# RWKV's second part as one pass over its chunks, and a 64-row product in both MLPs

## The chip, the cores and the metric

The kernel runs on one core of a Trainium2 chip. The metric is the device time of one execution in microseconds (us), less is better. Engines are named as the profile names them: PE (TensorE, matmuls) with PEld (its weight loads), DVE (VectorE), ACT (ScalarE), POOL (GpSimd) and SP (SyncE, which issues most loads). PE's two clock levels are 2.4 GHz (granted clock 1.00 in the rows) and 1.2 GHz (0.50).

## What is computed

Two layers of a decoder trunk on 256 tokens of width 2048, all in float32. The part that the change touches is layer 0, whose mixer puts sparse attention (NSA, 8 heads of 128) beside RWKV-7 (16 heads of 64), and the MLPs of both layers:

```
for layer in range(DEPTH):
    h = _rms_norm(x, norm_mix[layer])
    if layer % 2 == 0:
        u = h @ w_in_a[e]
        y_a = _nsa(u_nsa, ...)
        y_b = _rwkv7(u_rw, ...)
        y = jnp.concatenate([y_a, y_b], axis=-1) @ w_out_a[e]
    else: ...                                   # RG-LRU and HGRN2
    x = x + y
    x = x + _sq_relu_mlp(_rms_norm(x, norm_mlp[layer]), w_ff1[layer], w_ff2[layer])

def _rwkv7(...):                                # per head, state 64 x 64
    sa = einsum('bhij,bhj->bhi', state, a_t)
    state = state * w_t + sa * b_t + v_t * k_t
    y_t = einsum('bhij,bhj->bhi', state, r_t)
    ...
    y = ((y - mean) * lax.rsqrt(var + RW_LNX_EPS)) * lnx_w + lnx_b
    y = (y + bonus) * g

def _sq_relu_mlp(h, w1, w2):
    z = jax.nn.relu(h @ w1)
    return (z * z) @ w2
```

## The kernel before

**Projections and MLPs.** Activations lie transposed, channels on the 128 partitions, 256 tokens along a row. Each activation is held as two fp32r halves side by side (`hi|lo`, 512 columns), each weight is loaded as fp32 (512 KB a piece, issued by SP), cast on ACT to `wh` (L130) and its rest `wl` made on DVE (L132). A *unit* makes 128 output channels: 16 pairs of matmuls, each `wh` over 512 columns (L152) and then `wl` over 256 (L153). An MLP is 128 units, that is 2048 such pairs, and nothing else on PE but one mean-square product (L206) just ahead of it or in its first unit.

**Layer 0.** Up to about 310 us of the span PE runs the in-projection; `rwkv_a` makes, for each of 8 pairs of heads j, the operands of the chunked RWKV form (`rwp`, `pm`), writes them to DRAM, and gathers the 32x32 triangles `nb`, which DVE solves (`rw_solve`, L443 to L447) into `z_d` in DRAM. From about 310 to 466 us `rwkv_b` runs, four times, each for two pairs j and j+1: it loads `inv`, `pm`, `rwp` and `bg` (POOL issues these), makes the 64x64 inverses (`psh`, `psf`), and goes through 4 chunks of 64 tokens in turn: `psx` (state and scores times values), `psu` (the inverse applied), `pss` (state update), `psy` (output); at the end come the group norm (`pmn`, `pvr`) and the gate, into `yr`. Attention heads (lines above L555) and the units left over of the projection are interleaved. Then comes the out-projection (`mm_o`), the MLP of layer 0 (to about 1290), layer 1's mixer and out-projection (to about 1702) and its MLP.

**Order.** A scheduler fixes the order of each engine's instructions at build time, by dependences and priorities; on the chip each engine goes through its own in that order and waits where an operand is not there. Products of fp32 operands appear as two records each, fp32r ones as one. The size behind the buffers in a record, as `128*64`, is the part of the array (rows * columns) that it is set to; `128*128` is the whole.

Of the kernel before, what the change touches and what calls it, by code (L numbers as in the profile page):

```python
# [19 lines left out]
P = 128  # L20
# [34 lines left out]
RWP_N = 4 * 512 + 4  # L55
# [3 lines left out]
def kernel(  # L59
# [95 lines left out]
    def unit(src, mv, name, folded=False, tag=None, parts=None, pool=None):  # L155
# [76 lines left out]
    def layer0_mix():  # L232
        with ExitStack() as st:
            mx = st.enter_context(tc.tile_pool(name="mx", bufs=1))
            acc, hx = norm("a0")
            rwp_d = [dram.tile([P, 2, RWP_N], F32, name=f"rwp_d{j}") for j in range(4)]
            pm_d = [dram.tile([P, 2, 8, P], F32, name=f"pm_d{j}") for j in range(4)]
# [10 lines left out]
            with tc.tile_pool(name="pa", bufs=1) as pa:  # L248
# [39 lines left out]
                rwkv_a(pa, gate, hx, scaled_by(rstd), rwp_d, pm_d, nb, first, load_cw)  # L288
            with tc.tile_pool(name="pb", bufs=1) as pb, tc.tile_pool(name="pn", bufs=1) as pn:
                rw_solve(pb, nb, z_d)  # L290
                for j in range(0, 8, 2):
                    rwkv_b(pb, j, rwp_d, pm_d, z_d, yr)
# [17 lines left out]
    def rwkv_a(pa, gate, hx, scaled, rwp_d, pm_d, nb, first, load_cw):  # L310
# [26 lines left out]
        for j in range(8):  # L337
# [3 lines left out]
            rwp = tl("rwp", (P, RWP_N), 2, name=f"rwp_{j}")  # L341
            ar = rwp[:, 0:512].rearrange("p (c w t) -> p c w t", c=4, w=2)
            pm = tl("pm", (P, 8, P), 2, name=f"pm_{j}")
# [23 lines left out]
            A.copy(rwp[:, 1536:1540], w.rearrange("p (c t) -> p c t", c=4)[:, :, 63])  # L367
# [10 lines left out]
            with behind():  # L378
# [26 lines left out]
                V.tensor_mul(rwp[:, 1540:1796], psb[:, :T], v)  # L405
# [5 lines left out]
                A.copy(rwp[:, 1796:2052], psg[:, :T])  # L411
# [6 lines left out]
                A.copy(rwp[:, 1024:1536], ptv)  # L418
                A.copy(rwp[:, 512:1024], ptb)
# [6 lines left out]
                for q in range(2):  # L426
                    V.tensor_mul(
                        pm[:, 4 * q : 4 * q + 4], pps[q].rearrange("p (s t) -> p s t", s=4),
                        c_("pair")[:, None, :].to_broadcast([P, 4, P]))
                G.dma_start(pm_d[j // 2][:, j % 2], pm)  # L430
                for i in range(2):
                    G.dma_start(
                        nb[i * 64 + j * 8 : i * 64 + j * 8 + 8],
                        pm_d[j // 2][32 * i : 32 * i + 32, j % 2, :, 32 * i : 32 * i + 32].rearrange("s h t -> h s t"))
                G.dma_start(rwp_d[j // 2][:, j % 2], rwp)
# [14 lines left out]
    def rwkv_b(pb, j, rwp_d, pm_d, z_d, yr):  # L450


        def tl(tag, shape, bufs=1, name=None):
            return pb.tile(list(shape), F32, tag=tag, name=f"{tag}_{j}" if name is None else name, bufs=bufs)

        R = range(2)
        inv = tl("inv", (64, 2, 8, 64), 2)
        zat = tl("zat", (32, 2, 8, 32))
        pm = tl("pm", (P, 2, 8, P))
        rwp = tl("rwp", (P, 2, 1540))  # L460
        bg = tl("bg", (P, 2, 512))
        G.memset(inv, 0.0)
        inv16 = inv.rearrange("p r h t -> p (r h) t")
        for i in range(2):
            b0 = i * 64 + j * 8
            G.dma_start(inv16[32 * i : 32 * i + 32, :, 32 * i : 32 * i + 32], z_d[b0 : b0 + 16].rearrange("h r t -> r h t"))
        V.transpose(zat.rearrange("p r h t -> p (r h) t"), inv16[0:32, :, 0:32])
        G.dma_start(pm, pm_d[j // 2])
        G.dma_start(rwp, rwp_d[j // 2][:, :, 0:1540])
        G.dma_start(bg, rwp_d[j // 2][:, :, 1540:2052])  # L470
        ar = rwp[:, :, 0:512].rearrange("p r (c w t) -> p r c w t", c=4, w=2)
        bkt = rwp[:, :, 512:1024].rearrange("p r (c t) -> p r c t", c=4)
        uv = rwp[:, :, 1024:1536].rearrange("p r (c t) -> p r c t", c=4)
        wt, bv, gg = rwp[:, :, 1536:1540], bg[:, :, 0:256], bg[:, :, 256:512]
        psh = bank(f"psh_{j}")
        for r in R:
            for n in range(8):
                M.matmul(psh[32:64, (r * 8 + n) * 32 : (r * 8 + n + 1) * 32], pm[0:32, r, n, 32:64], zat[:, r, n], start=True, stop=True)
        hs_ = tl("hs", (64, 2, 8, 32))
        A.copy(hs_[32:64].rearrange("p r h t -> p (r h t)"), psh[32:64])  # L480
        psf = bank(f"psf_{j}")
        for r in R:
            for n in range(8):
                M.matmul(psf[0:32, (r * 8 + n) * 32 : (r * 8 + n + 1) * 32], hs_[32:64, r, n], inv[32:64, r, n, 32:64], start=True, stop=True)
        A.copy(inv[0:32, :, :, 32:64], psf[0:32].rearrange("p (r h t) -> p r h t", r=2, h=8))

        y = tl("y", (P, 2, T))
        y4 = y.rearrange("p r (c t) -> p r c t", c=4)
        s = None
        for c in range(4):  # L490
            psx = bank(f"psx_{j}_{c}")
            for r in R:
                if c:
                    M.matmul(psx[0:64, r * P : (r + 1) * P], ar[:, r, c, 0], s[:, r], start=True, stop=False)
                for h in range(2):
                    M.matmul(psx[0:64, r * P + h * 64 : r * P + h * 64 + 64], pm[64:128, r, 4 * h + c, 0:64],  # L496
                             uv[64:128, r, c, h * 64 : h * 64 + 64], start=c == 0, stop=c == 0 or h == 1)
            xv = tl("xv", (64, 2, P), name=f"xv_{j}_{c}")
            A.copy(xv.rearrange("p r t -> p (r t)"), psx[0:64, 0:T])
            psu = bank(f"psu_{j}_{c}")  # L500
            for r in R:
                for h in range(2):
                    M.matmul(psu[0:64, r * P + h * 64 : r * P + h * 64 + 64], inv[:, r, 4 * h + c], xv[:, r, h * 64 : h * 64 + 64],  # L503
                             start=True, stop=True)
            A.copy(uv[0:64, :, c], psu[0:64, 0:T].rearrange("p (r t) -> p r t", r=2))
            sn = None
            if c < 3:
                pss = bank(f"pss_{j}_{c}")
                for r in R:
                    M.matmul(pss[:, r * P : (r + 1) * P], bkt[:, r, c], uv[:, r, c], start=True, stop=True)  # L510
                sn = tl("st", (P, 2, P), 2, name=f"st_{j}_{c}")
                if c:
                    V.tensor_add(sn, pss[:, 0:T].rearrange("p (r t) -> p r t", r=2), s)
                for r in R:
                    V.scalar_tensor_tensor(sn[:, r], sn[:, r] if c else pss[:, r * P : (r + 1) * P], wt[:, r, c : c + 1], bones,
                                           ALU.mult, ALU.mult)
            psy = bank(f"psy_{j}_{c}")
            for r in R:
                rr = slice(r * 64, r * 64 + 64)
                if c:  # L520
                    M.matmul(psy[:, rr], s[:, r], ar[:, r, c, 1], start=True, stop=False)
                for h in range(2):
                    M.matmul(psy[h * 64 : h * 64 + 64, rr], uv[:, r, c, h * 64 : h * 64 + 64], pm[:, r, 4 * h + c, 64:128],
                             start=c == 0, stop=True)
            A.copy(y4[:, :, c], psy[:, 0:P].rearrange("p (r t) -> p r t", r=2))
            s = sn
        yf = y.rearrange("p r t -> p (r t)")
        pmn = bank(f"pmn_{j}")
        M.matmul(pmn, bones, yf, start=True, stop=True)
        V.scalar_tensor_tensor(yf, pmn, -1.0 / 64, yf, ALU.mult, ALU.add)  # L530
        sq = tl("ysq", (P, 512))
        A.activation(sq, yf, AF.Square)
        pvr = bank(f"pvr_{j}")
        M.matmul(pvr, bones, sq, start=True, stop=True)
        rs = tl("ysq", (P, 512), name=f"yrs_{j}")
        rsqrt_of(rs, pvr, 1.0 / 64, eps_ln, f"y{j}", pb)
        V.tensor_mul(yf, yf, rs)
        for r in R:
            A.activation(y[:, r], y[:, r], AF.Identity, bias=p_("lnx_b", j + r), scale=p_("lnx_w", j + r))
        V.tensor_add(y, y, bv)  # L540
        V.tensor_mul(y, y, gg)
        yj = yr[:, j : j + 2]
        A.copy(yj[:, :, :T], y)
        V.tensor_sub(yj[:, :, T:], y, yj[:, :, :T])
# [589 lines left out]
```

## Time and profile before

| | us |
|---|---|
| median of 3 runs | 2397.32 (2397.16 to 2398.94) |
| profiled execution, its own time | 2415.31 |
| its span, first to last instruction | 2413.5 |
| PE busy in it | 2390.6 (99%) |
| DVE busy | 1697.7 (70%) |
| ACT busy | 1243.7 (52%) |

The span is what the views of the profile divide up; its own time is 1.8 us more, and 18.0 us above the median of the runs. A PE record starts while the one before it still drains, so its length is no cost: costs on PE are read here from start to start.

### The profile page before, as it was taken

The numbers are of one execution on the slowest core, as the hardware profiler recorded it, in microseconds if no ns is written. First come the engines' busy times: TensorE is split into PE (matmuls) and PEld (weight loads), VectorE is DVE, ScalarE is ACT, GpSimd is POOL, SyncE is SP. The second block draws the span as 40 slices with busy tenths as digits, with TensorE's granted clock in tenths as the row PEclk, the third lists the DMA queues.
The fourth block names the chain that finished last, engine by engine and source line by source line (L and its number), as shares of the span: only waits on it lengthen the run. The fifth ranks groups of instructions, "written<-read, shape, count | busy, mean of one in ns | idle before, by whom it ended". The sixth has DMA issues, their size and how long they took to land.

```text
span 2413.5 us, 37947 instructions
## 1 busy us (share of the span) xinstructions
PE 2390.6 (99%) x14386; PEld 2072.1 (86%) x14386; DVE 1697.7 (70%) x3006; ACT 1243.7 (52%) x2152; POOL 44.9 (2%) x118
## 2 busy tenths in 40 slices
PE   8999999999999999999999999999999999999999
PEld 6888877798888888888888888889888888888888
DVE  7887865677676576576568888788777667667555
ACT  7554455555444444444456666675544444444443
POOL 0112010000000000000000000000000000000000
PEclk9999999999999999999999999999999999999999
DMA  7667743465555555655555444456556555656564
GB/s 263 212 216 228 246 139 105 155 209 183 190 184 186 188 184 187 188 185 187 187 176 187 150 151 153 154 168 217 185 191 191 189 188 191 192 187 190 191 199 134
DMA packets 125862, 446.77 MB, mean 185 GB/s; under 512 B 14192, under 2 KB 19952, under 8 KB 124016
## 3 DMA queue, kind: packets, MB, share of 16 engines
q1 hardware_dynamic: 115824, 414.06, 53.7%
q0 software_dynamic: 5456, 26.79, 3.1%
q10 hardware_dynamic: 4400, 3.50, 0.4%
q8 instruction: 114, 1.87, 0.3%
q14 instruction: 68, 0.56, 0.1%
HBM read 429.06 MB, written 15.22 MB: 184 GB/s over the span
## 4 chain that ended last, share of the span: by engine, by line
PE 93%; DVE 3%; DMA 2%; ACT 1%; issue 1%; POOL 0%; DVEq 0%; ACTq 0%; POOLq 0%
PE mm_f L152 39%; PE mm_f L153 20%; PE mm_i L152 13%; PE mm_i L153 7%; PE mm_o L153 2%; PE mm_o L152 1%; PE mm_o L149 1%; PE mm_o L150 1%; DVE wl_i L132 1%; PE hl L816 1%; PE pair L425 1%; DMA rwp<-rwp_d 1%; PE psx L496 0%; ACT wh_o L130 0%; PE psu L503 0%
## 5 line engine op out<-in xcount | busy, mean ns | idle before, releaser
L132 DVE TENSOR_TENSOR wl_f<-raw_f,wh_f 128x1024 fp32r<-128x1024 f32 x512 | 627.2, 1225 | 486.1 <-ACT wh_f L130 486.1
L130 ACT CAST wh_f<-raw_f 128x1024 fp32r<-128x1024 f32 x512 | 538.6, 1052 | 773.4 <-PE mm_f L152 566.8
L152 PE MATMUL mm_f<-hx_m,wh_f 128*128 128x512 f32 x2048 | 717.2, 395 | 0.0
L152 PE MATMUL mm_f<-z,wh_f 128*128 128x512 f32 x2048 | 717.1, 395 | 0.0
L152 PE MATMUL mm_i<-hx_a,wh_i 128*128 128x512 f32 x1536 | 563.9, 405 | 11.5 <-ACT wh_i L130 11.4
L153 PE MATMUL mm_f<-hx_m,wl_f 128*128 128x256 f32 x2048 | 574.8, 281 | 0.0
L153 PE MATMUL mm_f<-z,wl_f 128*128 128x256 f32 x2048 | 574.4, 280 | 0.0
L152 PEld LDWEIGHTS mm_f<-z,wh_f 128*128 128x128 f32 x2048 | 383.9, 187 | 90.0
L152 PEld LDWEIGHTS mm_f<-hx_m,wh_f 128*128 128x128 f32 x2048 | 383.9, 187 | 90.0
L153 PE MATMUL mm_i<-hx_a,wl_i 128*128 128x256 f32 x1536 | 447.6, 291 | 1.2 <-DVE wl_i L132 1.0
L153 PEld LDWEIGHTS mm_f<-hx_m,wl_f 128*128 128x128 f32 x2048 | 387.0, 189 | 0.1
L153 PEld LDWEIGHTS mm_f<-z,wl_f 128*128 128x128 f32 x2048 | 387.0, 189 | 0.0
L152 PEld LDWEIGHTS mm_i<-hx_a,wh_i 128*128 128x128 f32 x1536 | 289.8, 189 | 72.3 <-ACT wh_i L130 12.1
L153 PEld LDWEIGHTS mm_i<-hx_a,wl_i 128*128 128x128 f32 x1536 | 291.5, 190 | 9.3 <-DVE wl_i L132 4.0
L130 ACT CAST wh_i<-raw_i 128x1024 fp32r<-128x1024 f32 x192 | 201.3, 1049 | 188.9 <-PE mm_i L152 169.5
L132 DVE TENSOR_TENSOR wl_i<-raw_i,wh_i 128x1024 fp32r<-128x1024 f32 x192 | 234.5, 1222 | 80.6 <-ACT wh_i L130 76.4
L168 DVE TENSOR_TENSOR s_f<-mm_f,t_f 128x256 f32<-128x256 f32 x256 | 106.7, 417 | 3.0 <-ACT t_f L167 3.0
L132 DVE TENSOR_TENSOR wl_o<-raw_o,wh_o 128x1024 fp32r<-128x1024 f32 x64 | 78.3, 1223 | 32.6 <-ACT wh_o L130 32.3
L130 ACT CAST wh_o<-raw_o 128x1024 fp32r<-128x1024 f32 x64 | 67.2, 1050 | 63.3 <-issue 29.2
L167 ACT COPY t_f<-mm_f 128x256 f32<-128x256 f32 x256 | 93.2, 364 | 4.3 <-PE mm_f L153 4.3
L153 PE MATMUL mm_o<-ym,wl_o 128*128 128x256 f32 x256 | 72.6, 284 | 0.8 <-DVE wl_o L132 0.8
L942 DVE TENSOR_TENSOR s_f<-s_f,rstd_m 128x256 f32<-128x256 f32 x128 | 54.4, 425 | 4.4
(420 smaller groups left out, 2254.7 us busy)
## 6 DMA issues: line engine op xcount, KB each, us to landing
raw_f<-in_w_ff_dram SPq DMA_DIRECT2D x512, 512.0 KB, 4.5
raw_i<-in_w_in_dram SPq DMA_DIRECT2D x192, 512.0 KB, 4.1
raw_o<-in_w_out_dram SPq DMA_DIRECT2D x64, 512.0 KB, 4.2
rwp_d<-rwp POOLq DMA_DIRECT2D x8, 1026.0 KB, 7.1
rwp<-rwp_d POOLq DMA_DIRECT2D x4, 1540.0 KB, 10.7
cw<-in_cmp_w_dram SPq DMA_DIRECT2D x2, 2048.0 KB, 10.2
pm_d<-pm POOLq DMA_DIRECT2D x8, 512.0 KB, 6.3
pm<-pm_d POOLq DMA_DIRECT2D x4, 1024.0 KB, 5.3
```

Of the source, the lines that this page charges most:

```text
L130: A.copy(wh, raw)
L132: V.tensor_sub(wl, raw, wh)
L149: M.matmul(ps[:, :T], wh, mv[:, :T], start=first, stop=False)
L150: M.matmul(ps[:, :T], wh, mv[:, T:], start=False, stop=False)
L152: M.matmul(ps, wh, mv, start=first, stop=False)
L153: M.matmul(ps[:, :T], wl, mv[:, :T], start=False, stop=last)
L167: A.copy(t, ps[:, T:])
L168: V.tensor_add(s, ps[:, :T], t)
L425: M.matmul(pps[q][:, c * P : (c + 1) * P], bk[hs, c], ar[hs, c], start=True, stop=True)
L816: M.matmul(pl[:, x * T + i * P : x * T + (i + 1) * P], qk[:, ii], qk[:, ii], start=True, stop=True)
L942: V.tensor_mul(s, s, rstd)
```

## The change

**rwkv_b becomes one pass.** The four passes over two pairs of heads become one loop over the 4 chunks. Each chunk is done in two halves b = 0, 1 of four head pairs each, written as two generators that are stepped in turn, so that every kind of product stands for both halves before the next kind begins. All products other than those of the 32x32 triangles and of the group norm now use 128 rows by 64 columns of the array: operands that had 64 rows (`uv` under `psx`, `inv` and `xv` under `psu`) get zeros in the other rows, and the state `s` of two heads lies in a 128x128 tile with zeros off its diagonal blocks, multiplied head by head. The operands of a chunk are loaded for each half (`pm` 512 KB, `rw` 1 MB), with two buffers of each kind for the two halves; `inv` is gathered by 4 transfers for each half and chunk, 32 in all where there were 8. POOL zeroes `rw[0:64, :, 256:384]` after each load.

**rwkv_a** folds `lnx_w` and `lnx_b` into what it stores (one more DVE operation for each j; the ACT copy of the gate becomes a scaled one), keeps the decays in SBUF (`wts`), and stores chunk by chunk.

**narrow.** In both MLPs, in the unit of q = 0, k = 1, between the `wh` and the `wl` matmul of k = 4, a product of 64 rows of the identity by 128 columns goes to a PSUM bank that nothing reads.

```diff
+    def narrow(name):
+        ps = bank(f"nar_{name}")
+        tc.keep_in_program_order(M.matmul(ps[:, 0:P], ident[0:64], ident[0:64], start=True, stop=True))
...
             wh, wl = parts[k // 8]
+            if k == part_at:
+                M.matmul(ps, wh[:, k % 8], mv[k], start=False, stop=False)
+                narrow(name)
+                tc.keep_in_program_order(M.matmul(ps[:, :T], wl[:, k % 8], mv[k][:, :T], start=False, stop=False))
+                continue
             mm3(ps, wh[:, k % 8], wl[:, k % 8], mv[k], k == 0, k == KT - 1, folded)
...
-                V.tensor_mul(rwp[:, 1540:1796], psb[:, :T], v)
+                bv = tl("kf", name=f"bv_{j}")
+                V.tensor_mul(bv, psb[:, :T], v)
...
-                A.copy(rwp[:, 1796:2052], psg[:, :T])
+                A.activation(rwp[:, :, 448:512], pg4, AF.Copy, scale=p_("lnx_w", j))
+                V.scalar_tensor_tensor(
+                    rwp[:, :, 384:448], bv.rearrange("p (c t) -> p c t", c=4), p_("lnx_b", j), pg4, ALU.add, ALU.mult)
...
+        def chunk(c, b):
...
+            for i in range(2):
+                for q in range(2):
+                    G.dma_start(inv8[32 * i : 32 * i + 32, :, q, 32 * i : 32 * i + 32], zv[i, c, q, :, js])
+            pm = tl("pm", (P, 4, 2, P), 2, name=f"pmc_{n_}")
+            G.dma_start(pm, pm_d[:, js, c])
+            rw = tl("rw", (P, 4, 512), 2, name=f"rw_{n_}")
+            G.dma_start(rw, rwp_d[:, js, c])
+            G.memset(rw[0:64, :, 256:384], 0.0)
...
+            psx = bank(f"psx_{n_}")
+            for r in range(4):
+                if c:
+                    M.matmul(psx[0:64, r * P : (r + 1) * P], ac[:, r], s[:, r], start=True, stop=False)
+                for h in range(2):
+                    M.matmul(psx[0:64, r * P + h * 64 : r * P + h * 64 + 64], pm[:, r, h, 0:64],
+                             uv[:, r, h * 64 : h * 64 + 64], start=c == 0, stop=c == 0 or h == 1)
+            A.copy(xv[0:64].rearrange("p r t -> p (r t)"), psx[0:64])
+            yield
...
+            for r in range(4):
+                for h in range(2):
+                    o = psy[h * 64 : h * 64 + 64, r * 64 : r * 64 + 64]
+                    if c:
+                        M.matmul(o, s[:, r, h * 64 : h * 64 + 64], rc[:, r], start=True, stop=False)
+                    M.matmul(o, uv[:, r, h * 64 : h * 64 + 64], pm[:, r, h, 64:128], start=c == 0, stop=True)
...
         for c in range(4):
...
+            halves = [chunk(c, b) for b in range(2)]
+            while halves:
+                halves = [h for h in halves if next(h, 1) is None]
...
-                s = evac(unit(w_ff1[layer, q * KT + k], hx, n, pool=zraw), n)
+                s = evac(unit(w_ff1[layer, q * KT + k], hx, n, pool=zraw, part_at=4 if q == 0 and k == 1 else None), n)
```

The lines of `rwkv_b` that fall away are those of the function before.

**The order on PE, one chunk of RWKV.** Before, this stands on PE in the second chunk of the first pass, where `psx_1` takes the state `st` and the scores `pm`, and `psu_1` the inverse:

```order
L494 MATMUL psx_1_2850<-st_0_2841,rwp_2778 64x128
L496 MATMUL psx_1_2850<-rwp_2778,pm_2777 64x64 x2
L494 MATMUL psx_1_2850<-st_0_2841,rwp_2778 64x128
L496 MATMUL psx_1_2850<-rwp_2778,pm_2777 64x64 x2
L153 MATMUL mm_i_44_4601<-hx_a_0_93,wl_i_44_0_4606 128x256
L152 MATMUL mm_i_44_4601<-hx_a_0_93,wh_i_44_0_4604 128x512
...
L503 MATMUL psu_1_2859<-xv_1_2857,inv_2775 64x64 x4
```

After the change PE has at the second chunk (the halves are `_0_` and `_1_`; line numbers are those of the changed kernel, L511 is the state's product and L513 the scores'):

```order
L513 MATMUL psx_0_2862<-rw_0_2806,pmc_0_2804 64x64 x2
L511 MATMUL psx_0_2862<-s_2614,rw_0_2806 64x128
...
L513 MATMUL psx_0_2862<-rw_0_2806,pmc_0_2804 64x64 x2
L511 MATMUL psx_1_2876<-s_2615,rw_1_2827 64x128
L513 MATMUL psx_1_2876<-rw_1_2827,pmc_1_2825 64x64 x2
...
L520 MATMUL psu_0_2890<-xv_2612,inv_2610 64x64 x8
L520 MATMUL psu_1_2900<-xv_2613,inv_2611 64x64 x8
```

The products of two kinds still alternate, but all of them now have one shape of the array, and both halves follow each other without a matmul of a projection in between.

**The order on POOL, the loads of RWKV's second part.** Before, POOL's queue has, for the first two passes:

```order
L469 DMA rwp_2778<-rwp_d_96 128x2x1540
L466 DMA inv_2951<-z_d 32x16x32
L470 DMA bg_2779<-rwp_d_96 128x2x512
L462 MEMSET inv_3127 64x1024
L466 DMA inv_3127<-z_d 32x16x32
L468 DMA pm_2953<-pm_d_101 128x2048
```

After, it has for the second chunk, behind the zeroing for the first:

```order
L492 MEMSET rw_0_2806 64x4x128
L492 MEMSET rw_1_2827 64x4x128
L487 DMA inv_2610<-z_d 32x4x32 x4
L487 DMA inv_2611<-z_d 32x4x32
L489 DMA pmc_0_3010<-pm_d 128x4x256
L487 DMA inv_2611<-z_d 32x4x32 x3
L489 DMA pmc_1_3031<-pm_d 128x4x256
L491 DMA rw_0_3012<-rwp_d 128x4x512
L491 DMA rw_1_3033<-rwp_d 128x4x512
L492 MEMSET rw_0_3012 64x4x128
```

A chunk's `rw` is now loaded when the chunk before it has read its own to the end, and the zeroing of the first half stands behind the load of the second.

**The order on PE in the MLP of layer 0**, at the second unit, after the change (line 151 is `wh`, 152 `wl`; 165, 157 and 167 are the pair of k = 4 with the 64-row product in it):

```order
L152 MATMUL mm_f_0_0_1_6311<-hx_m_0_5197,wl_f_0_0_1_0_6316 128x256
L165 MATMUL mm_f_0_0_1_6311<-hx_m_0_5197,wh_f_0_0_1_0_6314 128x512
L157 MATMUL nar_f_0_0_1_6333<-con 128x128
L167 MATMUL mm_f_0_0_1_6311<-hx_m_0_5197,wl_f_0_0_1_0_6316 128x256
L151 MATMUL mm_f_0_0_1_6311<-hx_m_0_5197,wh_f_0_0_1_0_6314 128x512
```

Before there is nothing between the two matmuls of that pair. In the MLP of layer 1 it is the same; the 64-row product comes 25 instructions behind the mean-square product, and behind it 4055 matmuls of units follow one another on PE in either MLP.

## Rows read from the trace of the kernel before

**Rows 1.** The page's head: busy time and share of the span, instructions, by engine.

```profile
PE 2390.6 (99%) x14386; PEld 2072.1 (86%) x14386; DVE 1697.7 (70%) x3006; ACT 1243.7 (52%) x2152; POOL 44.9 (2%) x118
```

**Rows 2.** Windows: PE, PEld, DVE, ACT, POOL busy; PE clock, DMA share, GB/s.

```profile
0.00:310.00 310.00, 296.44 (x1781) 251.84 (x1781) 250.20 (x486) 172.01 (x313) 30.31 (x89) 1.00 0.70 231
```

**Rows 3.** The same view, of 600 us inside each MLP.

```profile
600.00:1200.00 600.00, 600.00 (x3399) 520.36 (x3398) 384.56 (x541) 269.58 (x378) 0.00 (x0) 1.00 0.59 186
1750.00:2350.00 600.00, 600.00 (x3464) 529.05 (x3463) 390.08 (x545) 273.68 (x382) 0.00 (x0) 1.00 0.60 191
```

**Rows 4.** Timeline of PE (start, length) around an L425 product ahead of `wl`.

```profile
82.16 1.16 PE L425 MATMUL pair<-rwp,bk 64*128 64x128 f32 x8
83.25 0.39 PE L153 MATMUL mm_i<-hx_a,wl_i 128*128 128x256 f32 x1
...
84.17 0.39 PE L152 MATMUL mm_i<-hx_a,wh_i 128*128 128x512 f32 x1
...
95.61 0.39 PE L152 MATMUL mm_i<-hx_a,wh_i 128*128 128x512 f32 x1
```

**Rows 5.** Timeline of PE around an L425 product ahead of `wh`.

```profile
225.77 1.57 PE L425 MATMUL pair<-rwp,bk 64*128 64x128 f32 x14
227.27 0.50 PE L152 MATMUL mm_i<-hx_a,wh_i 128*128 128x512 f32 x1
...
228.08 0.40 PE L152 MATMUL mm_i<-hx_a,wh_i 128*128 128x512 f32 x1
...
239.39 0.40 PE L152 MATMUL mm_i<-hx_a,wh_i 128*128 128x512 f32 x1
```

**Rows 6.** Timeline of PE, one `psx` of before.

```profile
365.61 0.40 PE L152 MATMUL mm_i<-hx_a,wh_i 128*128 128x512 f32 x1
365.94 0.43 PE L494 MATMUL psx<-st,rwp 128*64 128x128 f32 x2
366.30 0.44 PE L496 MATMUL psx<-rwp,pm 64*64 64x64 f32 x4
...
367.41 0.38 PE L153 MATMUL mm_i<-hx_a,wl_i 128*128 128x256 f32 x1
367.63 0.39 PE L152 MATMUL mm_i<-hx_a,wh_i 128*128 128x512 f32 x1
```

**Rows 7.** Timeline of PE, products of one shape, and `psu` of before.

```profile
374.44 0.67 PE L503 MATMUL psu<-xv,inv 64*64 64x64 f32 x8
375.05 0.70 PE L696 MATMUL o<-pts,vt 128*128 128x256 f32 x2
375.58 0.39 PE L697 MATMUL o<-pts,vt 128*128 128x128 f32 x2
375.81 0.61 PE L510 MATMUL pss<-rwp 128*128 128x128 f32 x4
```

**Rows 8.** The chain that ended last (start, length), ahead of and in RWKV.

```profile
307.76 3.59 DMA z_d<-nb
...
311.64 4.12 DMA inv<-z_d
...
345.88 0.65 POOL inv L466
```

**Rows 9.** Waits of 310 to 500 us: in total, times, longest.

```profile
PE psh L478 <- DVE zat L467: 1.1, 1, 1.1
...
PE mm_o L152 <- DVE yr L544: 0.9, 1, 0.9
```

**Rows 10.** DMA issues on the page: count, KB each, median us to landing.

```profile
rwp<-rwp_d POOLq DMA_DIRECT2D x4, 1540.0 KB, 10.7
...
pm<-pm_d POOLq DMA_DIRECT2D x4, 1024.0 KB, 5.3
```

**Rows 11.** A window of 5 us, columns as in Rows 2.

```profile
320.00:325.00 5.00, 5.00 (x48) 3.98 (x48) 1.60 (x12) 1.92 (x8) 0.00 (x0) 0.50 0.26 92
```

**Rows 12.** Groups of 310 to 470 us: busy, mean ns; idle before.

```profile
L559 DVE SCALAR_TENSOR_TENSOR nun_q<-qu,par,nrs_q 128x256 f32<-128x256 f32 x8 | 3.9, 481 | 5.0 <-ACT nrs_q L190 5.0
```

More of the change, by code (lines that the diff above doesn't have):

```diff
@@ L54 @@
 HG_LEVELS = (1, 2, 4, 8, 16, 32)
-RWP_N = 4 * 512 + 4
 @with_exitstack
@@ L235, in layer0_mix @@
             acc, hx = norm("a0")
-            rwp_d = [dram.tile([P, 2, RWP_N], F32, name=f"rwp_d{j}") for j in range(4)]
-            pm_d = [dram.tile([P, 2, 8, P], F32, name=f"pm_d{j}") for j in range(4)]
+            rwp_d = dram.tile([P, 8, 4, 512], F32, name="rwp_d")
+            pm_d = dram.tile([P, 8, 4, 2, P], F32, name="pm_d")
+            wts = mx.tile([P, 8, 4], F32, name="wts", bufs=1)
             z_d = dram.tile([P, 32, 32], F32, name="z_d")
@@ L287, in layer0_mix @@
                 first.append(unit(w_in0[3], hx, "i0_3", tag="gb"))
-                rwkv_a(pa, gate, hx, scaled_by(rstd), rwp_d, pm_d, nb, first, load_cw)
+                rwkv_a(pa, gate, hx, scaled_by(rstd), rwp_d, pm_d, wts, nb, first, load_cw)
             with tc.tile_pool(name="pb", bufs=1) as pb, tc.tile_pool(name="pn", bufs=1) as pn:
                 rw_solve(pb, nb, z_d)
-                for j in range(0, 8, 2):
-                    rwkv_b(pb, j, rwp_d, pm_d, z_d, yr)
+                rwkv_b(pb, rwp_d, pm_d, z_d, wts, yr)
                 kv = nsa_keys(pn, mx, hx, scaled_by(rstd), gate, cw, load_cw)
@@ L308, in scaled_by, with rwkv_a @@
         return scaled
-    def rwkv_a(pa, gate, hx, scaled, rwp_d, pm_d, nb, first, load_cw):
+    def rwkv_a(pa, gate, hx, scaled, rwp_d, pm_d, wts, nb, first, load_cw):
         def tl(tag, shape=(P, T), bufs=1, name=None):
@@ L366, in rwkv_a @@
             A.activation(wx, cs, AF.Exp, scale=DECAY)
-            A.copy(rwp[:, 1536:1540], w.rearrange("p (c t) -> p c t", c=4)[:, :, 63])
+            A.copy(wts[:, j], w.rearrange("p (c t) -> p c t", c=4)[:, :, 63])
             r = tl("r", bufs=2, name=f"r_{j}")
@@ L448, in rw_solve, with rwkv_b @@
         G.dma_start(z_d, nb)
-    def rwkv_b(pb, j, rwp_d, pm_d, z_d, yr):
+    def rwkv_b(pb, rwp_d, pm_d, z_d, wts, yr):
         def tl(tag, shape, bufs=1, name=None):
[L454 to L476, printed above, removed]
-            for n in range(8):
[L478 to L482, printed above, removed]
-            for n in range(8):
[L484 to L489, printed above, removed]
-        for c in range(4):
[L491 to L544, printed above, removed]
@@ new lines, in tl @@
+            return pb.tile(list(shape), F32, tag=tag, name=name or tag, bufs=bufs)
+        inv_ = [tl(f"inv{i}", (P, 8, 64)) for i in range(2)]
+        xv_ = [tl(f"xv{i}", (P, 4, P)) for i in range(2)]
+        s_ = [tl(f"s{i}", (P, 4, P)) for i in range(2)]
+        for t in inv_ + xv_ + s_:
+            G.memset(t, 0.0)
+        zv = z_d.rearrange("(i j c q) r t -> i c q r j t", i=2, j=8, c=4)
+        def chunk(c, b):
+            inv, xv, s = inv_[b], xv_[b], s_[b]
+            js = slice(4 * b, 4 * b + 4)
+            n_ = f"{c}_{b}"
+            inv8 = inv.rearrange("p (j q) t -> p j q t", q=2)
+            for i in range(2):
[6 more added lines that the diff above has]
+            G.memset(rw[0:64, :, 256:384], 0.0)
+            pm8 = pm.rearrange("p j q t -> p (j q) t")
+            zat = tl(f"zat{b}", (64, 8, 32), name=f"zat_{n_}")
+            V.transpose(zat[0:32], inv[0:32, :, 0:32])
+            psh = bank(f"psh_{n_}")
+            for n in range(8):
+                M.matmul(psh[32:64, n * 32 : (n + 1) * 32], pm8[0:32, n, 32:64], zat[0:32, n], start=True, stop=True)
+            A.copy(zat[32:64].rearrange("p n t -> p (n t)"), psh[32:64, 0:256])
+            yield
+            psf = bank(f"psf_{n_}")
+            for n in range(8):
+                M.matmul(psf[0:32, n * 32 : (n + 1) * 32], zat[32:64, n], inv[32:64, n, 32:64], start=True, stop=True)
+            A.copy(inv[0:32, :, 32:64], psf[0:32, 0:256].rearrange("p (n t) -> p n t", n=8))
+            ac, rc, uv = rw[:, :, 0:64], rw[:, :, 64:128], rw[:, :, 256:384]
+            yield
+            psx = bank(f"psx_{n_}")
[6 more added lines that the diff above has]
+            A.copy(xv[0:64].rearrange("p r t -> p (r t)"), psx[0:64])
+            yield
+            psu = bank(f"psu_{n_}")
+            for r in range(4):
+                for h in range(2):
+                    M.matmul(psu[0:64, r * P + h * 64 : r * P + h * 64 + 64], inv[:, 2 * r + h],
+                             xv[:, r, h * 64 : h * 64 + 64], start=True, stop=True)
+            A.copy(uv[0:64], psu[0:64].rearrange("p (r t) -> p r t", r=4))
+            yield
+            psy = bank(f"psy_{n_}")
+            for r in range(4):
+                for h in range(2):
+                    o = psy[h * 64 : h * 64 + 64, r * 64 : r * 64 + 64]
+                    if c:
+                        M.matmul(o, s[:, r, h * 64 : h * 64 + 64], rc[:, r], start=True, stop=False)
+                    M.matmul(o, uv[:, r, h * 64 : h * 64 + 64], pm[:, r, h, 64:128], start=c == 0, stop=True)
+            y = tl(f"yc{b}", (P, T), name=f"y_{n_}")
+            A.copy(y, psy[:, 0:T])
+            if c < 3:
+                yield
+                pss = bank(f"pss_{n_}")
+                for r in range(4):
+                    for h in range(2):
+                        M.matmul(pss[h * 64 : h * 64 + 64, r * 64 : r * 64 + 64],
+                                 rw[:, r, 128 + h * 64 : 128 + h * 64 + 64], uv[:, r, h * 64 : h * 64 + 64], start=True, stop=True)
+                for h in range(2):
+                    hs = slice(h * 64, h * 64 + 64)
+                    sd, pd = s[hs, :, h * 64 : h * 64 + 64], pss[hs, 0:T].rearrange("p (r t) -> p r t", r=4)
+                    if c:
+                        V.tensor_add(sd, sd, pd)
+                    V.tensor_mul(sd, sd if c else pd, wts[hs, js, c : c + 1].to_broadcast([64, 4, 64]))
+            yield
+            pmn = bank(f"pmn_{n_}")
+            M.matmul(pmn[:, 0:T], bones, y, start=True, stop=True)
+            V.scalar_tensor_tensor(y, pmn[:, 0:T], -1.0 / 64, y, ALU.mult, ALU.add)
+            sq = tl(f"ysq{b}", (P, T), name=f"ysq_{n_}")
+            A.activation(sq, y, AF.Square)
+            yield
+            pvr = bank(f"pvr_{n_}")
+            M.matmul(pvr[:, 0:T], bones, sq, start=True, stop=True)
+            rs = tl(f"ysq{b}", (P, T), name=f"yrs_{n_}")
+            rsqrt_of(rs, pvr[:, 0:T], 1.0 / 64, eps_ln, f"y{n_}", pb)
+            V.tensor_mul(y, y, rs)
+            y4 = y.rearrange("p (r t) -> p r t", r=4)
+            V.tensor_mul(y4, y4, rw[:, :, 448:512])
+            V.tensor_add(y4, y4, rw[:, :, 384:448])
+            cs = slice(c * 64, c * 64 + 64)
+            A.copy(yr[:, js, cs], y4)
+            V.tensor_sub(yr[:, js, T + c * 64 : T + c * 64 + 64], y4, yr[:, js, cs])
```

21 lines of the change are left out of this document (11 added, 10 removed).

## The prediction

> **What bounds the kernel now.** The page's head first: PE is busy for 2390.6 of the span's 2413.5 us [rows 1], so time can only come from PE doing the same with fewer or cheaper records, or from its few waits. The windows by stage come next. Up to 310 us DVE is at 250.2 of 310, the only place where another engine is near its limit [rows 2]. Inside the MLPs PE never stops, so there the rate of its records is the whole matter; and the same 600 us hold 3399 records in the first MLP and 3464 in the second [rows 3], although both stream the same pairs of `wh` and `wl`. A pair takes 600 / 1699.5 = 0.3530 us in the one and 600 / 1732 = 0.3464 in the other. The timeline of PE shows the same two periods elsewhere. After the L425 product (64 rows, another shape of the array) that has a `wl` behind it, 33 pairs lie between 84.17 and 95.61: 0.3467 each [rows 4]. After one with a `wh` behind it, 32 pairs lie between 228.08 and 239.39: 0.3534 each [rows 5]. So a run of pairs holds one of two periods until something other than a pair comes. Of the long runs in that stage that follow L425, all four with `wl` first have the short period and all three with `wh` first the long one; the rows are one of each. The mean-square product ahead of an MLP has the whole array's shape and fixes nothing: it stands between a `wh` and a `wl` both times, and the two MLPs differ. Last, the timeline in RWKV's second part, where the shape of the array changes all the time, and the chain and the waits there.
>
> **The forecast's base.** Durations are of one execution of 2415.3 us; the median of the runs is 2397.3, 0.75% lower. Differences taken from the one are set against the other without scaling (0.75% of 20 us is 0.15); a profile of the changed kernel should by the sum below be near 2395.7.
>
> **The 64-row product in the MLPs.** It is put where the short runs have theirs: narrow shape, `wl` next. If it works as L425 does [rows 4], the second MLP stays as it is, and the first falls to the short period for the 4055 matmuls behind the product and the 36 of the next projection up to its own mean-square product: 4091 / 2 = 2045 pairs by 0.3530 - 0.3464 = 0.0066, that is **-13.5**. Its own price comes from `psx` of before: from the `wh` at 365.61 to the `wh` at 367.63 are 2.02 us [rows 6], in which stand a `wh` and a `wl` (a pair, 0.35 [rows 3]), twice L494 with two records and twice L496 with four. Two records of 128 columns take 0.23 (375.58 to 375.81, one shape beside another of the same [rows 7]), one of 64 columns 0.058 (the eight of `psu` fill the 0.61 from 374.44 to 375.05 [rows 7], less one switch). That makes 0.35 + 2 x (0.23 + 0.23) = 1.27, and 0.75 is left for five changes of shape: **0.15 each**. A 64-row product between two whole ones is two changes and two records: 0.3 + 0.23 = 0.53, twice +1.1.
>
> **RWKV's second part, PE.** Along the order of PE from the first query norm to the MLP the shape changes 197 times before and 68 times after; 22 and 23 of them lie among products that are not RWKV's. What falls away is `psx` alternating between 64 and 128 rows, `psy` likewise, and the units between them. 129 x 0.15 = **-19.4**. Bounds: 0.14 to 0.17 for a change, at other spots of the kind, gives -18 to -22. That only the shape costs, not the change of operands, is seen where L697 meets L510: other operands, one shape, and 0.23 for two records, as inside a run [rows 7]. Against this go records. `psy` had 48 records of the state and 128 of the scores at 0.058, 10.2 us; with the state multiplied head by head it has 224 at 0.058, 13.0. `pss` had 48 of 128 columns at 0.115, 5.5, and has 96 of 64, 5.6. The others stay in number and columns, since a product costs its columns and not its rows [rows 6, 7]. **+2.9**.
>
> By the Trainium skill's page TensorEngine Tiling (Array Packing), section Theoretical Speedup, products with at most 64 rows can run in two tiles of the array at once, up to twice as fast, and padding them with zeros, as this change does, gives that away. Before, `psx` and `psu` have 256 such records; if they ran two at a time, padding would cost an estimated 256 x 0.058 / 2 = 7.4 us, and the sum would come to -12.2. The row says no: the eight of `psu` stand 0.058 apart, in 64 rows [rows 7].
>
> **RWKV's second part, waits.** The first wait is `psh` for the solved triangles: z_d's write starts at 307.76, `inv` lands at 315.76 (311.64 and 4.12) [rows 8], and PE stands for 1.1 [rows 9]. After the change DVE's order has three other operations ahead of the last step of the solve, a `wl` among them, about 2 us; and four gathers instead of two are issued ahead, 0.65 each [rows 8], 1.3. PE too comes later, by about 2. I take a wait of 2.3, **+1.2**. Then there are three chunk boundaries, which before did not exist in this form: a pass loaded the operands of its four chunks at once. Now `rw` of a chunk is free when the output chain of the chunk before has read it (two ACT and four DVE operations behind `pvr`, by 0.48 each as L559 [rows 12], some 3 us), then POOL issues (0.65), 1 MB lands twice, and POOL zeroes. By rows 1 MB lands in 5.3 (`pm`) to 10.7 us (1.5 MB of `rwp`) [rows 10]; I take 8.5 for two that share the queues. That is about 13 us from `pvr` to `psx`, where PE has by its order 8 to 9 us of other products (attention and units) and waits of its own before `psh` of the next chunk of about 1.3: some 1.2 left at `psx` beyond what hides it, 2.5 a boundary, **+7.5**; bounds 0 (landing in 5.3) to 5 a boundary (10.7). What falls away is the 0.9 of the out-projection for `yr` [rows 9] and 0.4 at the second pass: **-1.3**.
>
> **The first part.** Eight more DVE operations, as L559 with 0.48 us [rows 12], on an engine with 81% of that stage: 3.8 us if DVE is the limit there, 0 if not; I take half, **+1.9**.
>
> **The clock.** Behind the wait for `psh`, among the 32x32 products, PE's granted clock is 0.50 (1.2 GHz) in 320 to 325 us [rows 11], and about 5 us go there. The products and a wait ahead of them stay, so I let this stand as it is; -5 if it goes, as much again if one more such stretch comes at a boundary.
>
> **The sum.** MLPs -13.5 + 1.1 = -12.4; RWKV -19.4 + 2.9 + 1.2 + 7.5 - 1.3 + 1.9 = -7.2. Together -19.6: 2397.3 - 19.6 = 2377.7, **2378**.
>
> **Rivals.** (B) The MLPs give nothing. Either the runs that were timed already had the short period in the first MLP, or the 64-row product does not set it. For it speaks that the profiled execution is 18.0 us longer than the median, and 13.5 of these would be explained; against it, that all views of the profile show the state and nothing shows another. The time is then RWKV's share and the two products: 2397.3 - 7.2 + 1.1 = 2391. By the Trainium skill's page Runtime: NRT & Kernel Launch, section The ~15µs preamble/postamble breakdown, a profile's total is about 6.2 us above the execution time whatever the kernel; 11.8 of the 18.0 would then be left, near the 13.5. No row here shows which.
>
> (C) Slower: `rw` comes late. If the two loads and the zeroing behind them take not 8.5 but about 18 us, each boundary waits 12 instead of 2.5, and RWKV is 28.5 worse: 2377.7 + 28.5 = 2406. From 6.5 us more a boundary on (19.6 / 3) the gain is gone, from 8.1 on the kernel is measurably slower. For it: `rwp` takes 10.7 in the median [rows 10], and zeroing stands in line behind the other half's load; against it, these loads are a third smaller, and before the four passes hid theirs.
>
> (D) Both MLPs ran with the long period when timed. Then a second 13.5 comes: 2364. The profile's second MLP speaks against it.
>
> (E) The 64-row product sets the long period instead, in both: 2397.3 - 7.2 + 1.1 + 13.5 = 2405. The long runs had `wh` next, which this has not.
>
> **Chances.** The sum as argued 0.47, with its own range of 2368 to 2388 (boundaries from 0 to 5 each, -7.5 to +7.5; the first part and the clock for the rest); B 0.31; D 0.08; C 0.09; E 0.05. The range goes from D's 2364 to B with some boundary loss, 2399, and leaves out C, E and the tails. A measurement of this kernel tells about 0.2%, 4.8 us, from no change. Faster by more: the sum, D, and something over half of B (2391 is 0.26% below): 0.71. Within it: the rest of B and a little of C: 0.17. Slower: 0.12.
>
> **What would show it.** In the changed kernel's windows inside both MLPs about 3464 records for 600 us: then the product sets the short period; 3399 in either says it does not. The timeline of RWKV's second part should have `psx`, `psu` and `psy` of both halves as unbroken runs with 0.058 from record to record, and the stretch from the first query norm to the MLP some 8 us shorter. The waits should have `psx` for the zeroing or the load of `rw` at three places with 1 to 2 us each, and `psh` for `zat` at four. The prediction is wrong if these waits are of 8 us or more, if a change of operands inside one shape costs as much as one of shape, or if the first MLP's period was never long in the runs.

## The result, and the profile after

The changed kernel is slower: 2417.07 us in the median of four runs (2416.13 to 2418.48) against 2397.24 (2396.81 to 2398.94), a ratio of 1.0082 with a 95% interval of 1.0064 to 1.0099. The forecast was 2378 and its range ended at 2399.

The profiled execution says little by its span (2414.3 now, 2413.5 before), since before's was itself 18 us above its median. Its windows say where the time lies. 600 us inside each MLP of the changed kernel, which answer to [rows 3]:

```profile
600.00:1200.00 600.00, 600.00 (x3398) 520.30 (x3398) 384.43 (x540) 270.37 (x379) 0.00 (x0) 1.00 0.58 186
1750.00:2350.00 600.00, 600.00 (x3398) 520.29 (x3397) 382.21 (x534) 267.61 (x372) 0.00 (x0) 1.00 0.58 187
```

Both MLPs now have the long period, the second one too, which had 3464 records. The timeline of PE at the 64-row product shows nothing odd: two records, with `wl` behind them. From the `wh` ahead of it to the next are 0.95 us, so with the pair (0.35) off the product costs 0.60, where the forecast had 0.53.

```profile
552.71 0.39 PE L165 MATMUL mm_f<-hx_m,wh_f 128*128 128x512 f32 x1
553.03 0.48 PE L157 MATMUL nar_f<-con 64*128 64x128 f32 x2
553.44 0.39 PE L167 MATMUL mm_f<-hx_m,wl_f 128*128 128x256 f32 x1
553.66 0.39 PE L151 MATMUL mm_f<-hx_m,wh_f 128*128 128x512 f32 x1
```

RWKV's second part did get shorter. From the first query norm to the first mean-square product, by the rows of those two tiles (first start in each), before:

```profile
L206 PE MATMUL ms_m<-acc_m,con x4: 379/431/483, 562.2 to 1701.8; 128*128 128x256 f32 x4
...
L555 PE MATMUL nr_q<-nsq_q,con x16: 377/379/793, 310.0 to 462.7; 128*128 128x256 f32 x16
```

and after:

```profile
L215 PE MATMUL ms_m<-acc_m,con x4: 379/431/483, 548.2 to 1688.5; 128*128 128x256 f32 x4
...
L579 PE MATMUL nr_q<-nsq_q,con x16: 379/379/483, 315.7 to 448.8; 128*128 128x256 f32 x16
```

That is 252.2 us before and 232.5 after, but the stretch begins 5.7 later. The waits of PE from 240 to 560 us of the changed kernel:

```profile
PE psx L511 <- DMA rw<-rwp_d: 4.1, 3, 2.3
PE cmp L630 <- POOL upe L622: 3.7, 1, 3.7
PE psh L498 <- DVE zat L495: 2.0, 1, 2.0
PE pmn L548 <- DVE s L544: 1.0, 1, 1.0
```

The three waits for `rw` and the one at `psh` are those of the forecast, and near their size; of the four at `psh` that it looked for, only the first came. The second row is new: the compression of the attention's keys (`cmp`) waits for POOL. And PE's granted clock falls in the wait at `cmp` and again in the first wait of `psx`, which ends at 351 us:

```profile
260.00:265.00 5.00, 1.39 (x28) 1.27 (x32) 2.91 (x9) 0.51 (x1) 1.39 (x6) 0.72 0.47 184
265.00:270.00 5.00, 5.00 (x29) 4.19 (x22) 0.89 (x5) 1.79 (x7) 0.00 (x0) 0.60 0.58 202
350.00:355.00 5.00, 3.99 (x16) 3.02 (x17) 1.23 (x1) 0.97 (x5) 1.02 (x2) 0.66 0.70 265
```

Each row is at 0.50 (1.2 GHz) for a part of its 5 us; what it lacks of 1.00, times 5, is the work lost: 1.4, 2.0 and 1.7, 5.1 us in all (an estimate). The wait of 2.0 at `psh` was not followed by such a fall.

### The profile page after: what moved, and what is told of

It reads as the page before. It is cut to its first block, busy times and chain, and to the rows that moved or that the text cites. A ratio compares the mean times of both kernels' runs of the same rounds, so it can differ in the third digit from the quotient of the medians.

```text
span 2414.3 us, 38239 instructions
## 1 busy us (share of the span) xinstructions
PE 2383.6 (99%) x14502; PEld 2067.0 (86%) x14502; DVE 1699.9 (70%) x3026; ACT 1240.1 (51%) x2144; POOL 64.5 (3%) x156
## 4 chain that ended last, share of the span: by engine, by line
PE 91%; DVE 3%; DMA 3%; ACT 1%; issue 1%; POOL 0%; POOLq 0%; DVEq 0%; ACTq 0%
PE mm_f L151 40%; PE mm_f L152 20%; PE mm_i L151 12%; PE mm_i L152 6%; PE mm_o L152 2%; PE mm_o L151 2%; DMA rw<-rwp_d 1%; PE mm_o L148 1%; PE mm_o L149 1%; PE hl L840 1%; DVE wl_i L131 1%; PE pair L440 1%; DMA nb<-pm_d 0%; ACT wh_o L129 0%; DMA inv<-z_d 0%
## 5 line engine op out<-in xcount | busy, mean ns | idle before, releaser
L967 DVE SCALAR_TENSOR_TENSOR s_f<-s_f 128x256 f32<-128x256 f32 x128 | 54.4, 425 | 4.4
```

Of the source, the lines that this page charges most:

```text
L967: V.scalar_tensor_tensor(s, s, 0.0, s, ALU.max, ALU.mult)
```

## Experiments

Times are in us; before was timed on the same chip in each group of four. The 26, 23 and 26 times of before fall into two clusters each time, 2394 to 2402 and 2408 to 2411 (one time alone, 2406.43, lies between, with a granted clock of 0.995), and so a kernel is compared by clusters here, not by its median alone. The low cluster's median is 2395.5 in the first group. Two theories at the start: **P**, the 64-row product sets the long period in both MLPs; **R**, RWKV's new form is what costs the 20 us.

**The RWKV form alone** (`rwkv_only`).

```diff
-                s = evac(unit(..., pool=zraw, part_at=4 if q == 0 and k == 1 else None), n)
+                s = evac(unit(..., pool=zraw), n)
```

> The changed kernel without the 64-row product in both MLPs. Theory P (the MLPs' period): the runs of before that were timed have the short period in both MLPs, the 64-row product sets the long one in both (2 x 13.5 us and 1.1 for itself), and RWKV's new form saves about 7. Then this kernel takes about 2390, and 600 us inside each MLP hold about 3464 records, unless the mean-square product leaves one of them at 3399, which adds 13.5. Theory R (RWKV's second part is slower by some 20, the 64-row product does nothing): about 2416.

Ten runs: eight from 2384.76 to 2391.32, two at 2398.33 and 2401.45; ratio 0.9949 (0.9924 to 0.9975). The MLPs of the profiled one:

```profile
600.00:1200.00 600.00, 600.00 (x3463) 529.03 (x3462) 392.84 (x552) 276.87 (x391) 0.00 (x0) 1.00 0.57 190
1750.00:2350.00 600.00, 600.00 (x3464) 529.03 (x3463) 385.89 (x535) 272.15 (x376) 0.00 (x0) 1.00 0.57 192
```

R falls: without the product the new form is faster than before. The two slower runs, 11 and 14 above the median of the others, fit one MLP with the long period, as the expectation allowed for.

**The product alone, in both MLPs and in the first** (`product_only`, `product_mlp0`): before, with `narrow` and the changed `unit`, and `part_at=4 if q == 0 and k == 1`, the second with `and layer == 0`.

> The kernel before with the 64-row product in both MLPs and nothing else. Theory P: 2397.2 + 27.0 + 1.1 = 2425, with 3399 records in 600 us of either MLP. Theory R: 2397 to 2399, with the counts of before.

> The kernel before with the 64-row product in the MLP of layer 0 alone. Theory P, with both MLPs at the short period when before was timed: 2397.2 + 13.5 + 0.5 = 2411. If instead the runs of before that were timed had the long period in the first MLP as the profile shows: about 2398. Theory R: 2397 to 2398.

2424.01 (2423.14 to 2424.70) and 2410.43 (2409.13 to 2413.52), ratios 1.0084 (1.0051 to 1.0118) and 1.0029 (1.0007 to 1.0052). Each has one cluster only. `product_only` has 3398 records in 600 us of either MLP. From the one to the other are 13.6, the price of the long period in one MLP together with the second product (0.60). The profile of the second has the long period in the first MLP alone:

```profile
600.00:1200.00 600.00, 600.00 (x3398) 520.28 (x3397) 384.60 (x541) 269.30 (x378) 0.00 (x0) 1.00 0.55 186
1750.00:2350.00 600.00, 600.00 (x3464) 529.03 (x3463) 388.87 (x543) 274.14 (x381) 0.00 (x0) 1.00 0.57 191
```

So before's low cluster fits both MLPs short, and its high one, 14 above, one of them long; the profiled execution of the forecast had the long period in the first MLP.

**The product one place earlier** (`product_ahead_of_wh`).

```diff
-                M.matmul(ps, wh[:, k % 8], mv[k], start=False, stop=False)
                 narrow(name)
-                tc.keep_in_program_order(M.matmul(ps[:, :T], wl[:, k % 8], ...))
+                tc.keep_in_program_order(M.matmul(ps, wh[:, k % 8], mv[k], start=False, stop=False))
+                M.matmul(ps[:, :T], wl[:, k % 8], ...)
```

> The changed kernel with the 64-row product one place earlier, ahead of the wh matmul of k = 4 and not behind it. If the matmul that follows decides the period (as after the 64-row products of the first part, only turned round), both MLPs get the short period, 3464 records in 600 us, and the time is about 2390 + 1 = 2391. If any narrow product of this form sets the long period, 3399 records and about 2417, as the changed kernel.

2414.06 (2413.02 to 2419.23), ratio 1.0046 (1.0024 to 1.0068), 3399 and 3398 records: long in both. With two records it does not matter what follows.

**Eight records, in both halves of the rows or in one** (`eight_records`, `eight_one_half`).

```diff
-        ps = bank(f"nar_{name}")
-        tc.keep_in_program_order(M.matmul(ps[:, 0:P], ident[0:64], ident[0:64], ...))
+        ps = [bank(f"nar_{name}_{h}", t) for h, t in enumerate(("ga", "gb"))]
+        for i in range(4):
+            h = slice(64 * (i % 2), 64 * (i % 2) + 64)
+            tc.keep_in_program_order(M.matmul(ps[i % 2][:, i * P : (i + 1) * P], ident[h], ident[h], ...))
```

The second has `ident[0:64]` and one bank in all four.

> The changed kernel with four 64-row products (eight records, both halves of the array's rows in turn, two banks) where it has one. If the number of records or the half that was not loaded makes the single product set the long period, this one sets the short one, as the eight of the first part with wl behind them did: 3464 records in 600 us of both MLPs, 2387 + 2 = 2389. If a 64-row product in the middle of these units sets the long one whatever its number: 3399 and about 2418.

> The changed kernel with four 64-row products that all lie in the first 64 rows of the array (eight records, wl behind them). If the number of records makes the short period: 3464 in 600 us and about 2388. If it is that both halves of the rows are loaded in turn: 3399 and about 2418.

2387.60 (2385.80 to 2391.86) and 2391.79 (2386.99 to 2396.59), ratios 0.9939 (0.9911 to 0.9967) and 0.9960 (0.9940 to 0.9980): short in both. The nine times of the second follow the granted clock of the run: the four below 2390 have 0.998 or 0.999, the five above 2391 have 0.995 or 0.996. The timeline and the windows of the first, and the timeline of the second:

```profile
550.33 0.72 PE L159 MATMUL nar_f<-con 64*128 64x128 f32 x8
550.98 0.39 PE L169 MATMUL mm_f<-hx_m,wl_f 128*128 128x256 f32 x1
...
600.00:1200.00 600.00, 600.00 (x3463) 529.07 (x3462) 392.24 (x552) 277.53 (x391) 0.00 (x0) 1.00 0.56 190
1750.00:2350.00 600.00, 600.00 (x3464) 529.03 (x3463) 385.96 (x535) 272.78 (x376) 0.00 (x0) 1.00 0.57 192
...
557.08 1.16 PE L158 MATMUL nar_f<-con 64*128 64x128 f32 x8
558.17 0.39 PE L168 MATMUL mm_f<-hx_m,wl_f 128*128 128x256 f32 x1
```

It is not the half that was left out. Whether it is the number of records or the length of the interruption is not separated: from the first narrow record to `wl` are 0.41 us with two, 0.65 and 1.09 with eight. The last two numbers show something else: products that alternate between the two halves of the rows take 0.65, the same four in one half 1.09, so the two halves work side by side.

**Eight records ahead of `wh`** (`eight_ahead_of_wh`): the two edits above together.

> The changed kernel with the eight records of four 64-row products one place earlier, ahead of the wh matmul. If the matmul behind the narrow products decides the period, as after the eight of the first part (wh behind them: long, seven of seven; wl behind them: short), both MLPs are long: 3399 records in 600 us, about 2415. If eight records set the short one wherever they stand: 3464 and about 2388.

2416.21 (2414.48 to 2420.76), ratio 1.0066 (1.0042 to 1.0089), 3398 and 3399 records: long. With eight records the matmul behind them decides, as [rows 4] and [rows 5] said. In the MLPs this held each time, but it is no strict rule: the traces of the fourteen kernels have 98 runs of pairs behind the 64-row products of the first part, where the 51 with `wh` next all have the long period, and of the 47 with `wl` next 42 have the short and 5 the long one (one stands at 151.65 us in `product_only`).

**A product of the whole array** (`whole_array_product`): `ident` in place of `ident[0:64]`.

> The changed kernel with a product of 128 rows in place of the one of 64, so that the shape of the array does not change. If the change of shape sets the long period, this one leaves it to chance as the mean-square product does: times in clusters near 2386, 2399 and 2413. If any interruption at that place sets it: about 2416 in all runs.

Ten runs spread from 2397.74 to 2417.64, five below 2404 and five from 2409.59 up; the profiled one, 2417.64, has 3399 and 3398 records. By the times (of the others no profile shows the MLPs) one MLP is long in the first five and both in the rest, and none has two short ones, which eight of ten have in `rwkv_only`. So neither expectation came true as it stood: a product without a change of shape leaves the period open, but it too pushes towards the long one.

**Eight records in before** (`before_eight`).

> The kernel before with the eight records of four 64-row products behind the wh matmul in both MLPs, in place of nothing. If they fix the short period: all runs in one cluster near 2395.5 + 2 = 2397 to 2398, none of the second cluster near 2409 that the kernel before has. If the short period of the run with eight records was chance: two clusters again.

Eight of ten runs from 2396.45 to 2399.49, two at 2404.56 and 2408.63; ratio 1.0004 (0.9986 to 1.0021). The profiled run, 2396.45, has 3463 and 3464 records. The two are not of the high cluster: their granted clocks are 0.997 and 0.996, where the other eight have 1.000 and the runs of before's high cluster 0.999 or 1.000. A mean of 0.996 over 2407 us is some 10 us of work lost (an estimate), which puts 2408.63 near 2399. So the high cluster is gone.

**A change of shape, by itself** (`psx_128_rows`): before, with `psx`'s scores over all rows.

```diff
-                    M.matmul(psx[...], pm[64:128, r, 4 * h + c, 0:64], uv[64:128, r, c, ...], ...)
+                    M.matmul(psx[...], pm[:, r, 4 * h + c, 0:64], uv[:, r, c, ...], ...)
```

> The kernel before with psx's score products over 128 rows instead of 64 (with what lies in the other rows, so the output is another), which leaves psx in one shape of the array. 24 + 12 = 36 changes of shape go, and nothing else. At 0.15 us each as read from the rows of before: -5.4 us, seen best as the distance from the first query norm to the mean-square product of the first MLP (246.5 in both kernels with before's RWKV that were looked at). If a change costs half of that: -2.7; if nothing: 0.

The same two tiles:

```profile
L206 PE MATMUL ms_m<-acc_m,con x4: 379/431/483, 550.9 to 1689.8; 128*128 128x256 f32 x4
...
L555 PE MATMUL nr_q<-nsq_q,con x16: 377/379/483, 309.9 to 452.4; 128*128 128x256 f32 x16
```

550.9 - 309.9 = 241.0, where before's form with the clock at full has 246.7 (`product_mlp0`, 310.7 to 557.4). 5.7 / 36 = 0.16 for a change. The times agree: six from 2388.71 to 2392.37 and four from 2403.22 to 2405.45, each 4 to 6 below a cluster of before. The profiled run, 2403.22, is one of the four, and its MLPs have 3398 and 3463 records: here the higher cluster is seen to be the first MLP long. Inside `psx` the rows say the same: four score records take 0.37 from start to start in before, with a change of shape, and 0.23 here, without one:

```profile
366.30 0.44 PE L496 MATMUL psx<-rwp,pm 64*64 64x64 f32 x4
366.67 0.43 PE L494 MATMUL psx<-st,rwp 128*64 128x128 f32 x2
...
330.03 0.40 PE L496 MATMUL psx<-rwp,pm 128*64 128x64 f32 x4
330.26 0.39 PE L494 MATMUL psx<-st,rwp 128*64 128x128 f32 x2
```

That is 0.14 for a change, and 0.058 for a record of 128 rows, what the forecast read for one of 64: the padding itself costs nothing.

**The zeros in the first part** (`zeros_in_first_part`): `rwkv_only`, and

```diff
-            G.memset(rw[0:64, :, 256:384], 0.0)                            # in chunk
...
-                A.copy(rwp[:, :, 256:384], ptv...)                         # in rwkv_a
+                G.memset(rwp[0:64, :, 256:384], 0.0)
+                A.copy(rwp[64:P, :, 256:384], ptv[64:P]...)
```

It rests on POOL's timeline in the changed kernel, where the zeroing stands in the queue until its load has landed, and the small memset that `cmp` needs stands behind it:

```profile
244.67 0.75 POOL L491 DMA_DIRECT2D rw<-rwp_d  x1
254.24 0.52 POOL L492 MEMSET rw<- 64x512 f32 x1 [8.83 <-DMA rw<-rwp_d]
254.71 0.70 POOL L447 DMA_DIRECT2D nb<-pm_d  x1
262.22 0.52 POOL L492 MEMSET rw<- 64x512 f32 x1 [6.82 <-DMA rw<-rwp_d]
...
263.44 0.17 POOL L622 MEMSET upe<- 128x32 f32 x2
```

> The changed kernel without the 64-row product, and with the zeros of rw[0:64, :, 256:384] written once for each j in the first part, into what it stores, so that POOL zeroes nothing behind a load. If POOL's zeroing behind the 1 MB load is what holds the memset that the compression (cmp) waits for, the wait of PE there (2.2 to 3.7 us) goes, and with it up to 2 us at psh, since the last gather of nb no longer stands behind it: about 2381 to 2383 against 2385 to 2387 for the RWKV form alone. If the wait has another cause: 2385 to 2387.

2386.99 (2379.05 to 2388.95), ratio 0.9922 (0.9893 to 0.9950). The wait at `cmp` is gone, so its cause is shown. But `psh` waits 2.5, and PE's clock falls behind it, as in [rows 11]:

```profile
320.00:325.00 5.00, 4.98 (x52) 4.20 (x53) 4.03 (x20) 1.70 (x6) 0.00 (x0) 0.50 0.32 108
325.00:330.00 5.00, 5.00 (x53) 4.43 (x51) 1.97 (x8) 3.40 (x14) 0.00 (x0) 0.51 0.00 0
```

Two such windows at half clock are 5 us of work lost, about what was won; over the whole of this run (2388.34) the granted clock is 0.995, some 12 us (an estimate). The fastest run, 2379.05, is the one whose granted clock is 1.000; the other five have 0.995 to 0.998.

**Both mended** (`both_mended`): `eight_records` and `zeros_in_first_part` together.

> The changed kernel with eight records in place of the two in both MLPs, and with the zeros written in the first part so that POOL zeroes nothing behind a load. Both effects of the single changes together: short period in both MLPs, no wait of PE at cmp; 2380 to 2389 (the granted clock of 0.5 that followed the wait at psh in the run with the zeros alone takes 5 of it where it comes), all runs below the fastest of before.

2384.58 (2383.00 to 2391.43), ratio 0.9936 (0.9912 to 0.9959): faster than before and than the changed kernel in every run. In its profile `psh` waits 0.5 and the clock stays at 1.00 there, but the waits of `psx` for `rw` are 7.8 in all, with one fall of the clock behind the longest of them (0.66 in 405 to 410): part of what was won ahead of RWKV is waited for inside it.

## Why the prediction was wrong, step by step

**The 64-row product, -13.5: wrong, and the main cause.** The step "if it works as L425 does" failed. L425 has eight records, this product two, and the runs show that two set the long period whatever follows, while behind eight the next matmul decides. The size was near (13.6 an MLP with the product's own 0.60, so 13.0, against 13.5), the sign was not. It was named as rival E, with 0.05.

**The base: wrong too.** The sum took the first MLP's long period, as profiled, for that of the timed runs. They had the short one, by their times; that was the first half of rival B. So there was nothing to win in either MLP and two long periods to lose: `product_only` lies 28.5 above the low cluster of its group (2424.01 against 2395.5), the two products included. Of the 18.0 us between profile and median, the 13.6 of an MLP and the stretch at half clock (252.2 there against 246.7 with full clock, 5.5) explain all; they come to 19.1. The 6.2 us of the Trainium skill's page Runtime: NRT & Kernel Launch, section The ~15µs preamble/postamble breakdown, do not show here: the changed kernel's profiled execution, 2416.13, is itself one of its four timed runs.

**The clock, left as it is: wrong.** In the groups of the experiments 67 of the 75 runs of before have a granted clock of 1.000, so the stretch at half clock, too, belonged to the profiled execution and not to the usual run. Of the 67 runs of kernels with RWKV's new form 65 have less than 1.000: 0.996 to 0.998 in the four of the changed kernel and in the ten of `rwkv_only`. At 2400 us a mean of 0.997 is some 7 us of work lost (an estimate). It comes from the new form and not from the product: `product_only` has 1.000 in all five runs. The one run of `zeros_in_first_part` at 1.000, 2379.05, is 17 below before's low cluster (with the wait at `cmp` gone too), where `rwkv_only` is 8.4 below.

**RWKV, -7.2: right in sign, near in size by luck.** The total by clusters is -8.4 (eight runs of `rwkv_only`, median 2387.1, against 2395.5), but terms that were off make it up. From the query norm on 246.7 became 232.5, -14.2, where the sum had -19.4 + 2.9 + 1.2 + 7.5 - 1.3 = -9.1. The change of shape is 0.14 to 0.16 by its own run, against 0.15. The waits were over-priced: `psx` 4.1, `psh` 2.0, 1.0 and 0.5 at `pmn` and `pvr` and 0.5 in two small ones make 8.1, where before's form has 3.1 (`product_mlp0`, from 310 us on): +5.0 instead of +7.4. The clock takes 1.7 in this stretch. And the +2.9 for records has the wrong sign. In the changed kernel (the first three rows) the 32 records of `psu` take 1.87 up to the first of `psy`, 0.058 each, but the 64 of `psy` take 1.86 up to the first of `pss`, 0.029 each; in before (the last two rows) four of `psy`'s scores take 0.27 with a change of shape in it:

```profile
358.23 2.03 PE L520 MATMUL psu<-xv,inv 128*64 128x64 f32 x32
360.10 0.34 PE L529 MATMUL psy<-rw,s 128*64 128x64 f32 x4
...
361.96 1.42 PE L538 MATMUL pss<-rw 128*64 128x64 f32 x32
...
333.62 0.34 PE L523 MATMUL psy<-pm,rwp 128*64 128x64 f32 x4
333.89 0.43 PE L521 MATMUL psy<-rwp,st 128*128 128x64 f32 x2
```

`psu` writes one half of the columns; `psy`, and `pss` after the change, send the two heads to the two halves, which work side by side. So `psy` has 6.5 before (128 scores at 0.029, 48 of the state at 0.058) and 6.5 after (224 at 0.029), and `pss` falls from 5.5 to about 2.8: -2.7 instead of +2.9 (an estimate). Then -19.4 - 2.7 + 5.0 + 1.7 = -15.4, against -14.2. No run tried `psy` and `pss` alone.

Ahead of the query norm the sum had +1.9 for DVE; it was 2 to 6 in these profiles (312.3 to 315.7 against 309.2 to 310.7). POOL's queue, not one of the terms, accounts for it: without the zeroing behind the loads the query norm begins at 310.3 and 310.5 (`zeros_in_first_part`, `both_mended`), although the DVE operations are still there. With it, PE waits 2.2 to 3.7 at `cmp`, and the clock falls behind that.

**The sum that would have been right:** 2395.5 + 28.5 - 8.4 = 2415.6, from `product_only` and `rwkv_only`; measured 2417.07. The 1.5 left is within what the runs of one kernel differ by with their clocks.

**The other rivals.** C (late `rw`) is refuted: 4.1 in all three boundaries, where it needed 12 in each. D had the state of the MLPs the wrong way round.

## What to carry to other kernels

A period read from one profiled execution may be one of several that the same program has; before pricing a gain on it, see whether the timed runs cluster, and which cluster the profile belongs to. A precedent in the trace holds for what it has in full: eight records and two of the same shape, with the same matmul behind them, acted in opposite ways. Before a record is given a price, see which half of the array the ones beside it use: two halves can work at once. A change that adds waits to PE may cost clock as well: set the granted clock of each run beside its time. And an instruction that waits for a load should not stand in a queue that other engines draw on.

## What the runs showed of the hardware that was not expected

A run of alternating 512- and 256-column matmuls keeps one of two periods, 0.346 or 0.353 us a pair, over 2000 pairs, and what interrupts it sets which: two records of 64 rows the long one (all seven MLPs profiled with them), eight with the 256-column one next the short (all eight MLPs profiled, but 42 of 47 runs of pairs in the first part), eight with the 512-column one next the long, two records of the whole array either, by the times. Why is not settled; four and six records were not tried, nor was the number parted from the time they take. A change of the array's shape costs 0.14 to 0.16 us. 64-column products cost the same with 64 and with 128 rows (0.058 us a record), but those that alternate between two halves of the columns cost half (0.029, `psy`), and products of 64 rows that alternate between two halves of the rows take 0.65 us where they take 1.09 in one half.
